# Hybrid attention layer, second query group: normalisation three slots behind its projection, copy, low part and transposition five slots behind it

## Chip, cores and metric

The kernel runs on one core of a Trainium2 chip. The metric is the device time of one launch in microseconds (us), as a median over runs; lower is better. Engines are named as the profile names them: PE (matrix multiply) and PEld (its weight load), DVE (vector), ACT (activation), POOL (general purpose) and SP, whose queue issues most of the transfers.

## The reference

One layer over 1024 tokens of width 1024. After an RMS normalisation, one projection gives the columns of two head groups and their gates. Group A is attention with 8 query heads on 2 key/value heads; its queries and keys are normalised per head and turned by rotary tables. Group B is attention in a neighbourhood window with a learned bias. What matters here is how the queries of group A come about:

```python
h = _rmsnorm(x, norm_gain[l])
proj = h @ w_in[l]
q_a, k_a, v_a, g_a, q_b, k_b, v_b, g_b = jnp.split(proj, split_at, axis=-1)
q_a = _rmsnorm(q_a.reshape(b, s, A_HEADS, HEAD_DIM), q_norm_a[l])
...
q_a = q_a * cos + _rotate_half_axial(q_a) * sin
...
o_a = _gqa_blocked(q_a, k_a, v_a) * jax.nn.silu(g_a)
```

The gated outputs of both groups go through an output projection, are added to x and normalised.

## The kernel before

**Tiling.** All columns are cut into 17 weight groups of 256 columns (13 of the input projection, 4 of the output projection). Float32 operands are split into a high and a low float16 part, and each product is three matmuls. A projection tile is two blocks of 128 tokens by 256 columns in one PSUM bank: 48 matmuls of 128x256, given out in eight chunks of six (`proj_pair`, `chunks`, L494). The four tiles of a group are called tile 0 to tile 3 here. The projection tiles use two PSUM buffers in turn, so a tile's first chunk waits until the tile two before it has been read out.

**The order of the work.** `Flow.step` makes one *slot*. In a slot it runs what was booked for "pre", then the slot's attention work, then "mid", the vector jobs, "post", and a number of projection chunks (`fill`). `at(delay, pos, fn)` books work for a later slot. Nine slots of eight chunks come first. Then come 64 slots, numbered 0 to 63 here, each with one *unit* of group A: one head and 128 queries. Slot i makes the scores of unit i in PSUM (L725, L727; two buffers in turn), the row minimum on DVE (L732), the exponential on ACT (L734), the float16 copy on ACT (L735), the low part on DVE (L740, in the slot after) and a transposition by SP (L745); five slots later PE multiplies with the values (L757 to L759). Slots 0 to 3 carry five chunks each, later ones about 4.2. In what prints of the program `s_1_2` and `nm_1_2` belong to unit 6 (block 1, head 2), `s_2_0` to unit 8, and the digits at the end of a name are serial numbers.

Each engine works through its own instructions in order. Until slot 5 the order on ACT, DVE, POOL and SP is chosen by a scheduler; from slot 6 on (`HAND`) instructions stand as they are written. PE's order is written out throughout.

**The second query group** (weight group 2, `QA + 1`; heads 4 to 7, first used in slot 32). Its tile 0 ends in the slot before slot 0, tile 1 in slot 1, tile 2 in slot 3 and tile 3 in slot 4. Per tile, `norm_rope` books:

- `a`, one slot later: two reads out of PSUM on ACT (L541, L542)
- `b`, one slot later: sums and scale on DVE (L545, L546) and a power on POOL (L547)
- `c`, two slots later: the product with that power on DVE (L551), two half products with the sine table on POOL (L555), the product with the cosine table on DVE (L558), the sum on POOL (L559)

and `qa_gen` books, four slots later, the float16 copy on ACT (L574), the low part on DVE (L575) and the transposition on SP (L578).

**Work that shares the queues.** Weight groups 3 and 4 make the queries of group B; their tiles are read out by L628 (ACT) and L633 (DVE). Group 3's tile 0 ends in slot 6, and its tile 2, which takes the same PSUM buffer, begins with the last chunk of slot 8. A weight group is scaled before it is split: squares on ACT (L362), a sum over partitions on PE (L378), a factor from that sum on DVE (L380), a power on POOL (L381), then the high part on ACT (L404) and the low part on DVE (L409). For weight group 4 this falls into slots 7 to 9. PE's wait for the scores of unit i is on the exponential of unit i-2 (same buffer).

## Time and profile before

| what | value |
|---|---|
| median of 3 runs | 566.72 us (564.27 to 571.57) |
| profiled execution | 566.36 us |
| its span, first to last instruction | 564.5 us |
| PE busy | 515.5 us, 91% of the span |
| DVE busy | 446.0 us, 79% |
| ACT busy | 367.8 us, 65% |
| POOL busy | 157.2 us, 28% |

The span is what the engines' rows cover; the profiled execution took 1.86 us more than that. A row of the timeline gives the start, the busy time, engine, line, operation, output and inputs with shapes, how many instructions were merged, and in brackets the idle time before it with the engine that ended it. A row of the windows view gives, for a stretch of the span, the busy time of each engine with its count of instructions, the clock granted to PE (1.00 is full), and the use of the DMA engines.

### The profile page before, as it was taken

What the parts mean: (1) busy time and instruction counts of PE and PEld (TensorE: products, weight loads), DVE (VectorE), ACT (ScalarE), POOL (GpSimd) and SP (SyncE); (2) the same over time, 40 slices, a digit from 0 to 9 for tenths busy, and PEclk for the clock granted to TensorE, in tenths of its full rate; (3) what the DMA queues carried; (4) which work ended last, traced back from release to release, by engine and by line L of the source; (5) the groups of instructions that cost most, each with busy time, mean ns of one, the idle gap of its engine ahead of it and who ended that gap; (6) DMA issues with size and microseconds to landing.
All of it is one profiled execution on the core that took longest, in us unless ns stands there. A gap on an engine that the chain in (4) does not pass through costs nothing.

```text
span 564.5 us, 13778 instructions
## 1 busy us (share of the span) xinstructions
PE 515.5 (91%) x5583; PEld 402.4 (71%) x5583; DVE 446.0 (79%) x911; ACT 367.8 (65%) x583; POOL 157.2 (28%) x181
## 2 busy tenths in 40 slices
PE   2577989989999999999999999999998889998994
PEld 0456877767887555568888888887776667788883
DVE  4588788989887988778789887588987798988532
ACT  5546456958787759587696886367777568663211
POOL 2395887670000000000000022433821231224000
PEclk9979999999999999999999999999999998999998
DMA  8999549789999999998999899436586599996612
GB/s 242 220 181 234 122 71 210 125 143 191 203 228 174 175 216 193 193 187 173 211 197 180 189 165 214 129 68 132 105 188 105 117 255 230 181 154 139 215 38 75
DMA packets 244513, 95.47 MB, mean 169 GB/s; under 512 B 235489, under 2 KB 236001, under 8 KB 242530
## 3 DMA queue, kind: packets, MB, share of 16 engines
q1 hardware_dynamic: 240850, 73.89, 71.8%
q0 software_dynamic: 3312, 19.92, 12.2%
q8 instruction: 43, 0.70, 0.5%
q10 hardware_dynamic: 288, 0.79, 0.5%
q14 instruction: 20, 0.16, 0.1%
HBM read 29.56 MB, written 4.19 MB: 60 GB/s over the span
## 4 chain that ended last, share of the span: by engine, by line
PE 51%; DVE 9%; ACT 8%; issue 5%; DMA 4%; SPq 0%; POOL 0%; DVEq 0%; POOLq 0%; ACTq 0%
PE pj L494 19%; PE kb L494 7%; PE pjb L494 5%; PE s L725 4%; PE s L727 4%; ACT rq L838 3%; PE sb L494 3%; PE pv L758 3%; DMA ar<-ar 3%; PE pv L759 3%; PE pv L757 3%; ACT ar L840 3%; DVE ar L836 2%; DVE ar L845 2%; DMA x2b<-in_x_dram 1%
## 5 line engine op out<-in xcount | busy, mean ns | idle before, releaser
L494 PEld LDWEIGHTS <-hT 128*128 128x128 f16 x2112 | 204.9, 100 | 58.8 <-issue 16.2
L494 PE MATMUL pj<-whl,hT 128*128 128x256 f16 x1680 | 201.6, 278 | 20.9 <-DMA hT<-ar 7.8
L734 ACT ACTIVATE ar<-s,nm,sm 128x1024 f32<-128x1024 f32 x64 | 76.9, 1202 | 56.6 <-DVE nm L732 56.3
L732 DVE CUSTOM_DVE_ANT_0 ar<-s,sm 128x1024 bf16<-128x1024 f32 x64 | 82.0, 1281 | 33.9 <-PE s L727 33.6
L494 PEld LDWEIGHTS <-ar 128*128 128x128 f16 x768 | 74.6, 99 | 11.7 <-issue 2.6
L740 DVE TENSOR_TENSOR ar<-ar 128x1024 f16<-128x1024 f32 x64 | 79.5, 1242 | 1.4 <-ACT ar L735 1.4
L735 ACT ACTIVATE ar<-ar 128x1024 f16<-128x1024 f32 x64 | 67.6, 1057 | 2.1 <-DVE sum L764 0.3
L838 ACT ACTIVATE rq<-ar,nm 128x384 f32<-128x384 f32 (+1 forms) x64 | 34.1, 580 | 38.4 <-DVE nm L836 37.7
L494 PE MATMUL pjb<-whl,ar 128*128 128x256 f16 x408 | 47.4, 273 | 0.0
L494 PE MATMUL kb<-hT,whl 128*128 128x512 f16 x192 | 44.5, 379 | 0.0
L409 DVE SCALAR_TENSOR_TENSOR whl<-raw,sm,whl 128x512 f16<-128x512 f32 x52 | 38.7, 770 | 2.8 <-ACT whl L404 2.8
L758 PE MATMUL pv<-va,ar 128*128 128x64 f16 x384 | 40.1, 194 | 0.0
L757 PE MATMUL pv<-va,ar 128*128 128x65 f16 x384 | 40.1, 193 | 0.0
L759 PE MATMUL pv<-va,ar 128*128 128x65 f16 x384 | 39.9, 192 | 0.0
L757 PEld LDWEIGHTS <-ar 128*128 128x128 f16 x384 | 35.7, 97 | 5.5 <-issue 0.3
L758 PEld LDWEIGHTS <-ar 128*128 128x128 f16 x384 | 35.5, 97 | 5.5 <-issue 0.3
L725 PE MATMUL s<-kTa,rq 128*128 128x512 f16 x128 | 38.5, 383 | 0.4 <-ACT ar L734 0.4
L212 POOL DMA_DIRECT2D raw<-in_w_dram x11 | 6.7, 607 | 113.0 <-ACT ar L735 89.0
L845 DVE SCALAR_TENSOR_TENSOR ar<-rq,ar 128x768 f16<-128x768 f32 (+1 forms) x32 | 30.7, 959 | 7.9 <-ACT ar L840 7.5
L879 POOL TENSOR_TENSOR ar<-ar,qkg 128x256 f32<-128x256 f32 x16 | 18.5, 1157 | 65.0 <-DVE qkg L877 63.7
L759 PEld LDWEIGHTS <-ar 128*128 128x128 f16 x384 | 35.5, 99 | 0.0
L404 ACT ACTIVATE whl<-raw,sm 128x512 f16<-128x512 f32 x52 | 34.0, 709 | 1.4 <-POOL sm L381 1.4
(174 smaller groups left out, 978.4 us busy)
## 6 DMA issues: line engine op xcount, KB each, us to landing
raw<-in_w_dram POOLq DMA_DIRECT2D x11, 1024.0 KB, 7.7
raw<-in_wo_dram POOLq DMA_DIRECT2D x4, 1024.0 KB, 6.3
ar<-in_x_dram SPq DMA_DIRECT2D x7, 512.0 KB, 6.3
khh<-ar SPq DMA_DIRECT2D x16, 128.0 KB, 3.4
x2b<-in_x_dram POOLq DMA_DIRECT2D x4, 512.0 KB, 6.9
x<-in_x_dram POOLq DMA_DIRECT2D x4, 512.0 KB, 6.2
out_dram<-x2b SPq DMA_DIRECT2D x8, 256.0 KB, 4.2
out_dram<-x SPq DMA_DIRECT2D x7, 256.0 KB, 2.9
```

The source lines that it names most:

```text
L409: dve.scalar_tensor_tensor(wp[g][1][:, q], raw[g][:, q], col(S_ + g), wp[g][0][:, q], op0=OP.mult, op1=OP.subtract)
L494: pe.matmul(*o[0], **o[1])
L725: pe.matmul(s[:, c * 512:(c + 1) * 512], q, kTa[:, 4 * c:4 * c + 4, hh], start=True, stop=False)
L732: dve.tensor_tensor_reduce(out=hl[:, 1].bitcast(BF16), in0=s, in1=col(SHA).to_broadcast([P, 1024]), scale=col(NSA), scalar=3e38, op0=OP.ad ...
L734: act.activation(p32, s, AF.Exp, bias=nm, scale=col(SCA))
L735: at(0, "mid", lambda: act.activation(hl[:, 0], p32, AF.Copy))
L740: dve.tensor_tensor(hl[:, 1], p32, hl[:, 0], op=OP.subtract)
L757: pe.matmul(o, pt[:, kt], va[:, kt, hh, v_hi], start=kt == 0, stop=False)
L758: pe.matmul(o[:, :D], pt[:, kt], va[:, kt, hh, v_lo], start=False, stop=False)
L759: pe.matmul(o, pt[:, 8 + kt], va[:, kt, hh, v_hi], start=False, stop=kt == 7)
L838: act.activation(p32[:, e], t[:, e], AF.Exp, bias=nm, scale=-1.0)
L845: dve.scalar_tensor_tensor(hl[:, 1], p32, 2.0 ** 14, hl[:, 0], op0=OP.mult, op1=OP.subtract)
```

## The change

Two delays grow by one slot for the second query group alone: `c` is booked three slots behind the projection instead of two, and copy, low part and transposition five instead of four. No instruction is added, removed or altered.

```diff
         at(1, "pre", a)
         at(1, "post" if g == QA + 1 else "mid", b)
-        at(2 if g == QA + 1 else 1, "post", c)
+        at(3 if g == QA + 1 else 1, "post", c)
         done(qn)
...
             def fin(q):
-                d = 4 if hh else 2
+                d = 5 if hh else 2
                 at(d, "pre", lambda: act.activation(stg[:, :, :, a:a + D], q, AF.Copy))
```

PE's instructions stand in the same order as before. On the other engines rows move between slots 2 and 10.

The first place is ACT from the exponential of unit 4 to that of unit 6 (slots 4 to 6). Before:

```order
L734 ACTIVATE ar<-s_1_0_1090,nm_1_0_1095,sm 128x1024
L574 ACTIVATE ar<-ar 128x8x64
L541 ACTIVATE ar<-pj_3_1059 128x512
L542 ACTIVATE ar<-pj_3_1059 128x512
L735 ACTIVATE ar<-ar 128x1024
L734 ACTIVATE ar<-s_1_1_1135,nm_1_1_1140,sm 128x1024
L735 ACTIVATE ar<-ar 128x1024
L734 ACTIVATE ar<-s_1_2_1209,nm_1_2_1214,sm 128x1024
```

Now:

```order
L734 ACTIVATE ar<-s_1_0_1083,nm_1_0_1088,sm 128x1024
L542 ACTIVATE ar<-pj_3_1051 128x512
L574 ACTIVATE ar<-ar 128x8x64
L362 ACTIVATE va,wss_2_937<-raw_933 128x512
L735 ACTIVATE ar<-ar 128x1024
L734 ACTIVATE ar<-s_1_1_1134,nm_1_1_1139,sm 128x1024
L362 ACTIVATE va,wss_3_938<-raw_933 128x512
L735 ACTIVATE ar<-ar 128x1024
L734 ACTIVATE ar<-s_1_2_1202,nm_1_2_1207,sm 128x1024
```

Two squares of weight group 5 (L362) have moved in, from a place some three slots earlier; L541 of tile 3 has moved ahead of unit 4's exponential.

The second place is DVE from the low part of unit 5 (the first L740) to the row minimum of unit 8. Before:

```order
L740 TENSOR_TENSOR ar<-ar 128x1024
L551 TENSOR_TENSOR ar<-ar,nt_3_1129 128x512
L558 TENSOR_TENSOR ar<-ar,tabs 128x512
L732 ISA ar,nm_1_3_1281<-s_1_3_1276,sm 128x1024
L732 ISA nm_1_3_1281 128x1
L740 TENSOR_TENSOR ar<-ar 128x1024
L575 TENSOR_TENSOR ar<-ar 128x8x64
L633 SCALAR_TENSOR_TENSOR ar<-pj_0_1180,ar 128x2x64 x4
L380 TENSOR_SCALAR wss_0_871<-pv_101 128x1
L732 ISA ar,nm_2_0_1360<-s_2_0_1355,sm 128x1024
```

Now:

```order
L740 TENSOR_TENSOR ar<-ar 128x1024
L575 TENSOR_TENSOR ar<-ar 128x8x64
L551 TENSOR_TENSOR ar<-ar,nt_2_1050 128x512
L558 TENSOR_TENSOR ar<-ar,tabs 128x512
L732 ISA ar,nm_1_3_1275<-s_1_3_1270,sm 128x1024
L732 ISA nm_1_3_1275 128x1
L740 TENSOR_TENSOR ar<-ar 128x1024
L633 SCALAR_TENSOR_TENSOR ar<-pj_0_1172,ar 128x2x64 x4
L551 TENSOR_TENSOR ar<-ar,nt_3_1129 128x512
L558 TENSOR_TENSOR ar<-ar,tabs 128x512
L380 TENSOR_SCALAR wss_0_871<-pv_101 128x1
L732 ISA ar,nm_2_0_1357<-s_2_0_1352,sm 128x1024
```

Ahead of L633 the same kinds of rows stand as before, but L551 and L558 are now tile 2's; tile 3's pair has moved behind L633 and stands ahead of L380, the factor of weight group 4.

The third place is POOL from the power of tile 1 to the power of weight group 4 (L381). Before:

```order
L547 TENSOR_TENSOR nt_1_973<-nt_1_973,mh 128x8
L555 TENSOR_TENSOR ar<-ar,tabs 128x8x32 x2
L559 TENSOR_TENSOR ar<-ar 128x512
L547 TENSOR_TENSOR nt_2_1058<-nt_2_1058,mh 128x8
L555 TENSOR_TENSOR ar<-ar,tabs 128x8x32 x2
L559 TENSOR_TENSOR ar<-ar 128x512
L547 TENSOR_TENSOR nt_3_1129<-nt_3_1129,mh 128x8
L555 TENSOR_TENSOR ar<-ar,tabs 128x8x32 x2
L559 TENSOR_TENSOR ar<-ar 128x512
L381 TENSOR_TENSOR sm<-wss_0_871,mh 128x1
```

Now:

```order
L547 TENSOR_TENSOR nt_1_968<-nt_1_968,mh 128x8
L555 TENSOR_TENSOR ar<-ar,tabs 128x8x32 x2
L547 TENSOR_TENSOR nt_2_1050<-nt_2_1050,mh 128x8
L559 TENSOR_TENSOR ar<-ar 128x512
L547 TENSOR_TENSOR nt_3_1129<-nt_3_1129,mh 128x8
L555 TENSOR_TENSOR ar<-ar,tabs 128x8x32 x2
L559 TENSOR_TENSOR ar<-ar 128x512
L555 TENSOR_TENSOR ar<-ar,tabs 128x8x32 x2
L559 TENSOR_TENSOR ar<-ar 128x512
L381 TENSOR_TENSOR sm<-wss_0_871,mh 128x1
```

The powers of tiles 2 and 3 have moved ahead of their neighbours' products, and L381 still follows tile 3's L555 and L559, which on DVE now start behind L633. On ACT, L404 of weight group 4 still stands ahead of the exponential of unit 8, with a copy of tile 2 (L574, tile 3's before) ahead of both. On SP each L578 has moved behind one or two later transpositions of units.

## The prediction

> **What bounds the kernel now.** I read the windows of the trace first, to see where PE does not work, then PE's timeline there, and then the timelines of the engines it waits for. A window's columns are its length and the busy time of PE, PEld, DVE, ACT and POOL, then PE's granted clock.

> ```profile
> 120.00:130.00 10.00, 7.28 (x73) 5.26 (x70) 9.93 (x19) 6.65 (x9) 4.54 (x4) 0.83 0.77 146
> 130.00:140.00 10.00, 10.00 (x124) 8.36 (x122) 9.96 (x19) 7.60 (x10) 0.64 (x1) 1.00 1.13 188
> ...
> 300.00:350.00 50.00, 50.00 (x628) 41.15 (x626) 43.21 (x73) 36.34 (x44) 6.87 (x10) 1.00 0.97 191
> ```

> From 130 to 350 us, first and last window shown, PE is never idle, so whatever PE loses or gains before 130 arrives whole at 350, and I let it run through to the end. In 120 to 130 PE is busy for 7.28 of 10 us while DVE is busy for 9.93. This hole lies in the slots that the change rearranges.

> ```profile
> 102.20 0.59 PE L725 MATMUL s<-kTa,rq 128*128 128x512 f16 x2 [0.44 <-ACT ar L734]
> ...
> 114.17 0.59 PE L725 MATMUL s<-kTa,rq 128*128 128x512 f16 x2
> ...
> 118.49 0.59 PE L725 MATMUL s<-kTa,rq 128*128 128x512 f16 x2
> ...
> 120.09 2.78 PE L494 MATMUL pj<-whl,hT 128*128 128x256 f16 x24
> 125.59 1.44 PE L494 MATMUL pj<-whl,hT 128*128 128x256 f16 x6 [2.72 <-DVE wss L380]
> 126.82 1.06 PE L725 MATMUL s<-kTa,rq 128*128 128x512 f16 x2
> ...
> 132.07 0.59 PE L725 MATMUL s<-kTa,rq 128*128 128x512 f16 x2
> ...
> 136.29 0.59 PE L725 MATMUL s<-kTa,rq 128*128 128x512 f16 x2
> ```

> An L725 opens each PE slot; 118.49 is unit 8's, 132.07 unit 10's. A slot with four chunks takes 136.29 - 132.07 = 4.22 us; one with the sum over weight group 4 (L378) 118.49 - 114.17 = 4.32; a fifth chunk adds a quarter of the 2.62 between a group of 24 and the next row, 0.66. Slot 8 has five chunks and should take 4.88; it takes 8.33. Slot 9 takes 5.25 instead of 4.22. Together 3.45 + 1.03 = 4.48 us are lost: 2.72 of waiting, and about 1.76 because PE restarts slowly:

> ```profile
> 126.00:128.00 2.00, 2.00 (x8) 1.03 (x7) 2.00 (x4) 1.82 (x3) 0.15 (x1) 0.50 1.08 202
> ```

> The granted clock is 0.50 there. The chunk that waited is the first of group 3's tile 2. The row names L380, but the buffer is freed by the four L633 just ahead of it:

> ```profile
> 101.76 1.28 DVE L732 CUSTOM_DVE_ANT_0 ar<-s,sm 128x1024 bf16<-128x1024 f32 x1
> ...
> 106.55 1.28 DVE L732 CUSTOM_DVE_ANT_0 ar<-s,sm 128x1024 bf16<-128x1024 f32 x1
> ...
> 115.25 1.27 DVE L732 CUSTOM_DVE_ANT_0 ar<-s,sm 128x1024 bf16<-128x1024 f32 x1
> ...
> 119.22 0.69 DVE L551 TENSOR_TENSOR ar<-ar,nt 128x512 f32<-128x512 f32 x1 [1.54 <-POOL nt L547]
> 119.94 0.69 DVE L558 TENSOR_TENSOR ar<-ar,tabs 128x512 f32<-128x512 f32 x1
> 120.55 1.28 DVE L732 CUSTOM_DVE_ANT_0 ar<-s,sm 128x1024 bf16<-128x1024 f32 x1
> ...
> 121.75 1.22 DVE L740 TENSOR_TENSOR ar<-ar 128x1024 f16<-128x1024 f32 x1
> 122.90 1.75 DVE L575 TENSOR_TENSOR ar<-ar 128x512 f16<-128x512 f32 x1
> 124.58 0.87 DVE L633 SCALAR_TENSOR_TENSOR ar<-pj,ar 128x128 f16<-128x128 f32 x4
> 125.37 0.14 DVE L380 TENSOR_SCALAR wss<-pv 128x1 f32<-128x1 f32 x1
> ```

> The L732 shown are those of units 3, 4, 6 and 7. DVE stands still for 1.54 us at tile 3's L551, which waits for POOL's power, and spends 1.75 on an L575 that takes 0.69 elsewhere. So L633 comes too late.

> **The change part by part.** It adds no instruction; everything follows from the order.

> *What goes.* Ahead of L633 stands tile 2's L551 instead of tile 3's. Tile 2's power was ready long before, so the 1.54 goes; and ahead of unit 6's L732 stand an L575, an L551 and an L558 less. If that were all, L633 would be in time and PE would get back 4.48 us.

> *What comes first: unit 4's exponential is later.* ACT's rows:

> ```profile
> 98.78 0.63 ACT L362 ACTIVATE va<-raw 128x512 bf16<-128x512 f32 x1
> ...
> 99.39 1.05 ACT L735 ACTIVATE ar<-ar 128x1024 f16<-128x1024 f32 x1
> ...
> 107.87 1.21 ACT L734 ACTIVATE ar<-s,nm,sm 128x1024 f32<-128x1024 f32 x1 [1.09 <-DVE nm L732]
> 108.97 0.62 ACT L574 ACTIVATE ar<-ar 128x512 f16<-128x512 f32 x1
> 109.49 0.59 ACT L541 ACTIVATE ar<-pj 128x512 f32<-128x512 f32 x1
> 109.97 0.60 ACT L542 ACTIVATE ar<-pj 128x512 f32<-128x512 f32 x1
> 110.45 1.06 ACT L735 ACTIVATE ar<-ar 128x1024 f16<-128x1024 f32 x1
> 111.39 1.22 ACT L734 ACTIVATE ar<-s,nm,sm 128x1024 f32<-128x1024 f32 x1
> ...
> 126.18 2.56 ACT L404 ACTIVATE whl<-raw,sm 128x512 f16<-128x512 f32 x4 [1.42 <-POOL sm L381]
> 128.65 1.19 ACT L734 ACTIVATE ar<-s,nm,sm 128x1024 f32<-128x1024 f32 x1
> ```

> From start to start an L734 takes 1.10, L574 0.52, L542 0.48, L735 0.94, L362 0.61 and four L404 2.47; on DVE an L740 takes 1.15, L551 0.72, L558 0.61, L732 1.20, four L633 0.79. Unit 3's and unit 4's L732 start 4.79 apart; between them there is now one L740 and one small L546 (0.2) more and an L575 (0.69) less: 5.45. Unit 3's own L732 has an L575 newly ahead of it, with two L362 taken off ACT in that place: I put it at 102.2 to 102.5. Unit 4's L732 then starts at 107.7 to 108.0 (was 106.55), its exponential 1.32 later as now, ending at 110.2 to 110.5. PE, which no longer waits the 0.44 at 102.20, wants that buffer at 109.5: a wait of 0.7 to 1.0 that is not there today.

> *Unit 6.* ACT runs L734, L542, L574, L362 and L735 from 109.0 to 109.3 on: 1.10 + 0.48 + 0.52 + 0.61 + 0.94 = 3.65, so 112.7 to 113.0, up to 0.5 more where L574 waits for tile 1's sum, which on POOL now stands behind tile 2's power. An L740 later, at 113.9 to 114.7, unit 6's L732 starts (was 115.25). ACT ends L734, L362 and L735 of unit 5 at 115.4 to 116.1.

> *L633.* From there DVE does L740, L575, L551, L558, L732, L740: 1.15 + 0.69 + 0.72 + 0.61 + 1.20 + 1.15 = 5.52. L633 starts at 120.9 to 121.6 and ends by 122.4, where PE reaches the waiting chunk at about 123.2 (L725 at 110.3 to 110.6, then 4.22 and 4.32 to 119.0, and 4.2 into slot 8). The old wait goes.

> *What is late next.* Tile 3's L551 and L558, which stood ahead, now stand behind L633, and POOL can start tile 3's L555 and L559 only then. Behind these on POOL stands L381, behind it on ACT the four L404, behind them unit 8's exponential, and behind that the scores of unit 10 on PE. POOL's rows:

> ```profile
> 120.04 1.86 POOL L555 TENSOR_TENSOR ar<-ar,tabs 128x256 f32<-128x256 f32 x2 [0.86 <-ACT ar L628]
> 121.97 2.13 POOL L559 TENSOR_TENSOR ar<-ar 128x512 f32<-128x512 f32 x1
> 125.59 0.56 POOL L381 TENSOR_TENSOR sm<-wss,mh 128x1 f32<-128x1 f32 x1 [1.49 <-DVE wss L380]
> ```
> ```profile
> 104.44 2.77 POOL L555 TENSOR_TENSOR ar<-ar,tabs 128x256 f32<-128x256 f32 x2 [0.87 <-DVE ar L551]
> 107.29 1.27 POOL L559 TENSOR_TENSOR ar<-ar 128x512 f32<-128x512 f32 x1
> ```

> Today L559 is over at 124.1, 1.49 us before L381 can start, so L381 waits only for L380. Now: L551 starts at 121.7 to 122.4 and takes 0.72; L555 takes 1.86 to 2.77, L559 1.27 to 2.13, L381 0.56: 126.1 to 128.6. With L404 (2.47) and the exponential (1.19) unit 8's buffer is free at 129.8 to 132.3, and up to 1.06 later if an L575 is again held up as at 122.90 (1.75 instead of 0.69). PE wants it at 119.0 + 4.88 + 4.22 = 128.1. So there is a new wait of 1.7 to 5.2 us, about as long as the one that goes. L380 itself moves to 123.0 to 123.8 and ends by 124, and PE's first product of the second block with the values waits for it at 124.7: no cost, with 0.7 us to spare.

> *The sum*, by the start of unit 10's scores, today 132.07: 129.8 to 133.4. L575 and L558 on DVE and tile 2's and 3's L555 and L559 on POOL now run against each other just there, so I take the upper part, 132.0. Then PE restarts slowly, as at 126 today, which I price with the same 1.76, less about 0.2 because slot 10 has no fifth chunk. That is 132.0 - 132.07 + 1.6 = +1.5 us; from -0.7 (129.8, slow restart) or -2.3 (129.8, no slow restart) to +2.9. The first, short wait (0.7 to 1.0) is inside, since PE waits for unit 8 in any case. Span 564.5 + 1.5 = 566.0; the profiled execution takes 1.86 us more than its span and lies 0.36 under the median shown, so I predict **567.9 us**, with 564.1 to 569.3 as this case's own range. That is within 2% (11.3 us) of 566.72, about what a measurement of this kernel can tell from no change.

> What speaks on the slow restart: PE's idle of 2.72 us was followed by a clock of 0.50. [...]

> **The rivals.**

> *The stall goes and no other comes*: -4.48, that is 561.9 us. It needs unit 8's exponential over by 128.1, so L381 at 123.8 and tile 3's L551 by 119.9 at the latest, about as early as today, though it now stands behind L633. It could be had if POOL's rows were shorter than any shown. Halfway lies a wait too short to lower the clock: -2.3, 564.1.

> *POOL and DVE hold each other up* (slower). L575's 1.75 starts at 122.90 inside L559's 2.13, and both are long against 0.69 and 1.27. If each of the pairs that now meet does this, L575 and L558 ahead of L633 give 1.06 + 0.5, and tile 3's rows take their longest:

> ```profile
> L555 POOL TENSOR_TENSOR ar<-ar,tabs x24: 449/730/1710, 39.8 to 121.2; 128x256 f32<-128x256 f32 x16, 128x128 f32<-128x128 f32 x8
> L559 POOL TENSOR_TENSOR ar<-ar x12: 723/1266/2266, 41.4 to 122.0; 128x512 f32<-128x512 f32 x8, 128x256 f32<-128x256 f32 x4
> ```

> Two of 1.71 and one of 2.27 are 0.8 more than I counted: 132.3 + 1.6 + 0.8 = 134.7, so +2.6 + 1.6 = +4.2, 570.6 us. It decides as soon as L381 starts after 127.8 (then unit 10 starts after 132.07). [...]

> *The change does nothing that can be seen*: the wait moves from slot 8 to slot 10 at the same length. Tile 0's L551 does not even move in the order. Then 4.48 goes and 4.48 comes: 566.4 us.

> **How the numbers follow.** New wait a little longer than the old: 0.42, 567.9. No new stall: 0.17, 561.9 to 564.1. POOL and DVE in each other's way: 0.21, 570.6. Nothing: 0.20, 566.4. All four lie within 2%; beyond it only something I don't see. The runs shown spread over 7.3 us, so I add some 2 us on either side of 564.1 and 570.6: 562.0 to 573.0. Faster by over 2% (under 555.4) 0.02, slower by over 2% (over 578.1) 0.03, within 0.95.

> **What would show it.** In the changed profile the first chunk of group 3's tile 2 has no wait on DVE, and tile 3's L551 no wait on POOL; PE's wait named L734 lies before unit 10's scores and is 2 to 5 us long, with a granted clock near 0.5 right behind it, and a short one before unit 6's. L404 waits 2 to 4 us for POOL's L381, and POOL works without a gap from tile 3's L555 to L381. I am wrong if L381 still starts right behind L380 with POOL idle before it; if PE shows no wait over 1.5 us between 105 and 140; or if the total differs while these waits are as said, in which case the difference comes from behind 350 us.

## The result and the profile after

| | before | changed |
|---|---|---|
| median of 13 runs each | 566.68 us (564.27 to 571.57) | 572.71 us (571.26 to 588.16) |
| profiled execution | 566.36 us | 572.71 us |
| its span | 564.5 us | 570.9 us |

The ratio of the changed kernel to the one before is 1.0085, 95% interval 1.0056 to 1.0114: slower by less than 2%. The median is 4.8 us over the 567.9 forecast and just inside its upper bound of 573.0. Two later comparisons of the same two programs gave 1.0043 (1.0009 to 1.0078) and 1.0063 (1.0023 to 1.0103). Medians here and below are of all runs; the ratios leave out runs over 1.5% above the fastest of their program, and the profiled execution of n_after3 below (579.21 us) is one of those, so that it enters no mean.

First the windows of the changed kernel's trace, with the columns as in the prediction:

```profile
120.00:130.00 10.00, 10.00 (x124) 8.37 (x122) 9.93 (x18) 4.48 (x6) 7.81 (x6) 1.00 1.01 198
130.00:140.00 10.00, 6.44 (x58) 4.84 (x57) 8.14 (x16) 7.92 (x11) 1.20 (x2) 0.83 0.64 111
...
300.00:350.00 50.00, 50.00 (x625) 41.14 (x623) 44.68 (x75) 35.53 (x42) 6.17 (x9) 1.00 0.95 188
```

The hole has moved. 120 to 130 us, where PE lost 2.72 us, is full; 130 to 140 has PE busy for 6.44 of 10 us. PE's timeline of the changed kernel, the first scores of units 6, 10, 11 and 12:

```profile
113.60 0.59 PE L725 MATMUL s<-kTa,rq 128*128 128x512 f16 x2 [1.36 <-ACT ar L734]
...
134.94 0.59 PE L725 MATMUL s<-kTa,rq 128*128 128x512 f16 x2 [3.56 <-ACT ar L734]
...
140.76 0.59 PE L725 MATMUL s<-kTa,rq 128*128 128x512 f16 x2
...
145.08 0.59 PE L725 MATMUL s<-kTa,rq 128*128 128x512 f16 x2
```

Both waits are on an exponential (L734) of the unit two before. Slot 10 takes 140.76 - 134.94 = 5.82 us, 1.6 more than a slot with four chunks, and behind the wait the clock is low for one stretch:

```profile
134.94:135.40 0.46, 0.46 (x3) 0.22 (x3) 0.00 (x0) 0.46 (x1) 0.00 (x0) 1.00 0.01 2
135.40:138.80 3.40, 3.40 (x34) 2.46 (x33) 2.79 (x7) 3.37 (x6) 0.00 (x0) 0.50 0.09 19
138.80:142.00 3.20, 3.20 (x36) 2.52 (x35) 3.20 (x5) 1.86 (x3) 0.00 (x0) 0.99 1.13 210
```

What unit 8's exponential waits for, on DVE, POOL and ACT:

```profile
124.22 0.87 DVE L633 SCALAR_TENSOR_TENSOR ar<-pj,ar 128x128 f16<-128x128 f32 x4
125.01 0.97 DVE L551 TENSOR_TENSOR ar<-ar,nt 128x512 f32<-128x512 f32 x1
126.01 0.69 DVE L558 TENSOR_TENSOR ar<-ar,tabs 128x512 f32<-128x512 f32 x1
...
127.89 1.22 DVE L740 TENSOR_TENSOR ar<-ar 128x1024 f16<-128x1024 f32 x1
129.03 1.76 DVE L575 TENSOR_TENSOR ar<-ar 128x512 f16<-128x512 f32 x1
```
```profile
126.11 1.86 POOL L555 TENSOR_TENSOR ar<-ar,tabs 128x256 f32<-128x256 f32 x2 [0.68 <-ACT ar L574]
128.05 2.19 POOL L559 TENSOR_TENSOR ar<-ar 128x512 f32<-128x512 f32 x1
130.20 1.01 POOL L381 TENSOR_TENSOR sm<-wss,mh 128x1 f32<-128x1 f32 x1
```
```profile
131.24 2.56 ACT L404 ACTIVATE whl<-raw,sm 128x512 f16<-128x512 f32 x4 [5.14 <-POOL sm L381]
133.70 1.18 ACT L734 ACTIVATE ar<-s,nm,sm 128x1024 f32<-128x1024 f32 x1
```

L633 comes in time and tile 3's L551 behind it waits for nothing. POOL then works through tile 3's L555, L559 and weight group 4's L381 without a gap, ACT stands for 5.14 us before L404, and unit 8's exponential ends as PE's wait ends.

**Where the 6.4 us of span are.** Compared from PE's weight loads, which stand in the same order in both programs, unit 3's scores start 2.72 us later (100.18 against 97.46), before any row that the change moved has been waited for. From there to unit 12's scores, the stretch that the change rearranges, it takes 145.08 - 100.18 = 44.90 us against 43.15: +1.75. From unit 12's scores to 300 us of the trace before nothing differs (0.01), and another 1.95 arise in group B, between 430 and 500 us of the trace before. Two of PE's waits there in the changed kernel, and one each of two later profiles of the program before (n_before, then n_before2):

```profile
452.20 0.32 PE L815 MATMUL sb<-khh,qTb 128*128 128x384 f16 x1 [4.13 <-DVE nm L836]
...
472.48 0.20 PE L865 MATMUL pvb<-ar 128*128 128x65 f16 x1 [3.03 <-DMA ar<-ar]
```
```profile
448.15 0.48 PE L815 MATMUL sb<-khh,qTb 128*128 128x384 f16 x1 [4.13 <-DVE nm L836]
```
```profile
465.37 0.24 PE L865 MATMUL pvb<-ar 128*128 128x65 f16 x1 [5.45 <-DMA ar<-ar]
```

In the first profile of the program before, the wait on L836 was 2.74 us and none was on L865. So neither the longer wait on L836 nor a transfer that is late at L865 is anything that the change made; the unchanged program has both, in some executions.

### The profile page after: what moved, and what is told of

It is laid out like the page before. It is cut to its first block, busy times and chain, and to the rows that moved or that the text cites. A ratio compares the mean times of both kernels' runs of the same rounds, so it can differ in the third digit from the quotient of the medians.

```text
span 570.9 us, 13780 instructions
## 1 busy us (share of the span) xinstructions
PE 515.9 (90%) x5583; PEld 402.8 (71%) x5583; DVE 445.7 (78%) x911; ACT 367.4 (64%) x583; POOL 155.4 (27%) x181
## 4 chain that ended last, share of the span: by engine, by line
PE 51%; ACT 10%; DVE 7%; issue 5%; DMA 4%; POOL 0%; DVEq 0%; POOLq 0%; ACTq 0%
PE pj L494 18%; PE kb L494 7%; PE pjb L494 6%; PE s L727 4%; PE s L725 4%; ACT rq L838 4%; DMA ar<-ar 4%; PE sb L494 3%; ACT ar L840 3%; PE pv L758 3%; PE pv L759 3%; PE pv L757 3%; DVE ar L836 2%; DVE ar L845 2%; ACT rest L362 1%
## 5 line engine op out<-in xcount | busy, mean ns | idle before, releaser
L494 PEld LDWEIGHTS <-hT 128*128 128x128 f16 x2112 | 204.6, 99 | 57.7 <-DMA hT<-ar 17.6
L494 PE MATMUL pj<-whl,hT 128*128 128x256 f16 x1680 | 202.0, 279 | 19.9 <-DMA hT<-ar 9.9
L734 ACT ACTIVATE ar<-s,nm,sm 128x1024 f32<-128x1024 f32 x64 | 76.9, 1201 | 55.0 <-DVE nm L732 52.9
L732 DVE CUSTOM_DVE_ANT_0 ar<-s,sm 128x1024 bf16<-128x1024 f32 x64 | 81.9, 1281 | 33.4 <-PE s L727 33.1
L494 PEld LDWEIGHTS <-ar 128*128 128x128 f16 x768 | 75.2, 100 | 12.6 <-issue 2.8
L740 DVE TENSOR_TENSOR ar<-ar 128x1024 f16<-128x1024 f32 x64 | 79.3, 1240 | 3.6 <-ACT ar L735 3.6
L735 ACT ACTIVATE ar<-ar 128x1024 f16<-128x1024 f32 x64 | 67.6, 1057 | 2.1 <-DVE ar L740 0.3
L494 PE MATMUL pjb<-whl,ar 128*128 128x256 f16 x408 | 47.4, 273 | 0.0
L494 PE MATMUL kb<-hT,whl 128*128 128x512 f16 x192 | 44.5, 379 | 0.0
L725 PE MATMUL s<-kTa,rq 128*128 128x512 f16 x128 | 38.0, 379 | 4.9 <-ACT ar L734 4.9
L404 ACT ACTIVATE whl<-raw,sm 128x512 f16<-128x512 f32 x52 | 34.0, 709 | 5.1 <-POOL sm L381 5.1
```

What stands on the lines that cost most here:

```text
L494: pe.matmul(*o[0], **o[1])
L725: pe.matmul(s[:, c * 512:(c + 1) * 512], q, kTa[:, 4 * c:4 * c + 4, hh], start=True, stop=False)
L732: dve.tensor_tensor_reduce(out=hl[:, 1].bitcast(BF16), in0=s, in1=col(SHA).to_broadcast([P, 1024]), scale=col(NSA), scalar=3e38, op0=OP.ad ...
L734: act.activation(p32, s, AF.Exp, bias=nm, scale=col(SCA))
L735: at(0, "mid", lambda: act.activation(hl[:, 0], p32, AF.Copy))
L740: dve.tensor_tensor(hl[:, 1], p32, hl[:, 0], op=OP.subtract)
```

## The experiments

Each ratio is from runs on the same chip as those of the program before. "Stretch" is the time from the start of unit 3's scores to the start of unit 12's in the profiled execution, "waits" are PE's in it.

| run | ratio to before (95%) | median | stretch | waits in it |
|---|---|---|---|---|
| the two programs first compared: before | 1 | 566.68 | 43.15 | 0.44 and 2.72 |
| changed | 1.0085 (1.0056 to 1.0114) | 572.71 | 44.90 | 1.36 and 3.56 |
| n_before | 0.9994 (0.9955 to 1.0034) | 567.41 | 42.72 | 2.74 |
| n_before2 | 1.0014 (0.9981 to 1.0047) | 569.24 | 43.00 | 0.48 and 2.73 |
| n_after | 1.0043 (1.0009 to 1.0078) | 571.31 | 42.08 | 2.31 |
| n_after2 (one run) | - | 571.81 | 44.58 | 1.36 and 3.55 |
| n_after3 | 1.0063 (1.0023 to 1.0103) | 572.34 | 43.30 | 1.17 and 3.54 |
| c3_f4 | 1.0023 (0.9986 to 1.0060) | 571.26 | 44.50 | 0.48 and 3.94 |
| c2_f5 | 0.9974 (0.9931 to 1.0017) | 568.31 | 38.00 | none |
| t3_6 | 0.9966 (0.9931 to 1.0001) | 565.17 | 38.00 | none |
| t3_6b | 0.9966 (0.9937 to 0.9995) | 566.69 | 38.00 | none |
| sq5 | 1.0029 (0.9993 to 1.0066) | 569.35 | 41.85 | 2.08 |
| c2_f5_sq5 | 0.9980 (0.9944 to 1.0015) | 567.18 | 38.00 | none |
| t3_6_sq5 | 0.9962 (0.9928 to 0.9996) | 566.04 | 38.00 | none |

The median of before was 568.64 us beside n_before, n_after, c3_f4 and c2_f5 (35 runs), 567.96 beside t3_6, sq5, c2_f5_sq5 and n_after2 (29), and 568.42 beside the other four (35).

The stretch without any wait is 38.00 us, five times out of five. Every other entry is 38.00 plus the waits plus 0.6 to 2.1 us, which I put down to the low clock behind the waits for the most part: 38.00 + 0.44 + 2.72 leaves 1.99 for before, 38.00 + 1.36 + 3.56 leaves 1.98 for the changed kernel.

### The parts of the change alone

The products one slot later, the copies in their old place:

```diff
-        at(2 if g == QA + 1 else 1, "post", c)
+        at(3 if g == QA + 1 else 1, "post", c)
```

> Only the normalisation (c) is moved, to three slots; copy, low part and transposition stay at four. ACT's order is then that of the kernel before, and tile 3's products stand behind L633 and ahead of L381 as in the change. Theory of the prediction (L381 behind tile 3's products costs): the wait before unit 10's scores is there with 3 to 5 us, the one before unit 6's is gone, and the middle stage takes 44.0 to 45.5 us; ratio 1.002 to 1.008. Rival (the later copies on ACT cost, with the wait before unit 6's scores as their mark): the middle stage takes 42.5 or less, ratio 0.998 or less.

Measured: the long wait before unit 10 is there, as long as with the whole change, and none before unit 6. The two rows of tile 2's and tile 3's copy on ACT, and PE's wait:

```profile
122.37 0.63 ACT L574 ACTIVATE ar<-ar 128x512 f16<-128x512 f32 x1 [3.65 <-POOL ar L559]
...
129.41 0.63 ACT L574 ACTIVATE ar<-ar 128x512 f16<-128x512 f32 x1 [3.68 <-POOL ar L559]
```
```profile
133.63 1.01 PE L725 MATMUL s<-kTa,rq 128*128 128x512 f16 x2 [3.94 <-ACT ar L734]
```

So the later products suffice to make the new wait. That it is L381 which passes it on, this run doesn't show: tile 3's copy on ACT (the second L574) waits for the same L559 itself and stands ahead of L404. PE also waits 1.28 us before unit 3 here, ahead of the stretch; there ACT waited 4.07 us for weight group 5's load, of which more below.

The copies one slot later, the products in their old place:

```diff
-                d = 4 if hh else 2
+                d = 5 if hh else 2
```

> Only copy, low part and transposition are moved, to five slots; the normalisation stays at two. Tile 3's products stay ahead of L633, so L381 waits only for L380, and tile 2's L575 goes behind L633. Theory of the prediction: the wait before unit 6's scores (1.4 us) is there, none before unit 10's, at most 1 us in slot 8, and the middle stage takes 40.0 to 41.5 us; ratio 0.994 to 0.997. Rival (the later copies cost): 44 to 45 us as in the change, ratio 1.003 or more. Theory B above (any such change makes the rest slower by 4 us): ratio 1.002 or more with a middle stage of 41.

Measured: the old wait goes and no other comes, not even the expected one before unit 6. L381 starts early, and PE is never idle:

```profile
121.44 2.14 POOL L559 TENSOR_TENSOR ar<-ar 128x512 f32<-128x512 f32 x1
123.54 0.56 POOL L381 TENSOR_TENSOR sm<-wss,mh 128x1 f32<-128x1 f32 x1
```
```profile
120.00:130.00 10.00, 10.00 (x122) 8.15 (x121) 9.93 (x21) 8.60 (x13) 4.02 (x4) 1.00 1.11 177
130.00:140.00 10.00, 10.00 (x138) 8.25 (x137) 9.96 (x22) 7.17 (x8) 1.21 (x2) 1.00 1.03 196
```

Of the two lines of the change, the second by itself takes the stall away, and the first makes the new one. The stretch is 5.15 us shorter than in the program before, better than expected; the time is not. That no wait stands before unit 6 belongs to this execution: ACT waited only 0.90 us for a load that had made it wait 2.62 us in the trace before (more on it below). ACT's order is that of the changed program, which has that wait in its three executions with a late load, so I would expect it here too with a late load; no profile shows it.

### L381 ahead of tile 3's products

The change as it is, with tile 3 alone another slot later:

```diff
-        at(3 if g == QA + 1 else 1, "post", c)
+        at((4 if up == 3 else 3) if g == QA + 1 else 1, "post", c)
...
-                d = 5 if hh else 2
+                d = (6 if up == 3 else 5) if hh else 2
```

> The changed program with tile 3's last step and its copy, low part and transposition one slot later still (normalisation four slots behind its projection, copy six behind), the other three tiles as in the change. That puts the power L381 on POOL ahead of tile 3's products L555 and L559 and behind those of tile 2. Theory (the long wait before unit 10 comes from L381 standing behind two tiles' products): L381 starts some 4 us earlier against unit 8's scores, the high parts L404 follow it, and the wait before unit 10 falls from 2.3 to 3.6 us to under 0.5 us; in its place up to 1.5 us of waiting in slot 10's last chunk, which needs tile 3's transposition. From unit 3's scores to unit 12's: 38 to 41 us instead of 42.1 and 44.9 in the two executions of the changed program. Rival (the wait comes from the exponentials being late on ACT and DVE as a whole, and the power's place decides little): the wait before unit 10 stays at 2 us or more and the stretch at 42 to 45 us.

POOL's rows, and ACT's high parts behind them:

```profile
119.62 2.13 POOL L559 TENSOR_TENSOR ar<-ar 128x512 f32<-128x512 f32 x1
121.72 0.56 POOL L381 TENSOR_TENSOR sm<-wss,mh 128x1 f32<-128x1 f32 x1
127.30 1.86 POOL L555 TENSOR_TENSOR ar<-ar,tabs 128x256 f32<-128x256 f32 x2 [5.02 <-ACT ar L735]
```
```profile
121.79 0.63 ACT L574 ACTIVATE ar<-ar 128x512 f16<-128x512 f32 x1
122.33 2.54 ACT L404 ACTIVATE whl<-raw,sm 128x512 f16<-128x512 f32 x4
```

L381 stands between tile 2's L559 and tile 3's L555, L404 no longer waits for it, and the wait is gone, with nothing in its place (I had allowed 1.5 us in slot 10's last chunk). This settles that L381's place behind tile 3's products makes the wait before unit 10: the changed program has 2.31 us of it even in the execution with the least waiting for the load, 1.05 us (n_after, below), and here ACT waited 1.68.

### What sets the size of the wait

The changed program unchanged, three times more:

> The changed kernel, unchanged, for a second profile. Both theories: the middle stage 44.9 within 0.5, with the wait of 3 to 4 us before the scores of unit 10 and one of 1.4 before unit 6's. Theory A: the first and last stage lie elsewhere than 100.2 and 425.8, by a us or two, on either side. Theory B: again 100.2 and 425.8 within 0.5. Median 572 to 573 under both, ratio 1.008 to 1.011.

> The changed program itself, once more, for a third profile. Theory of the load: the sum of the waits before unit 6 and before unit 10 goes with ACT's wait for weight group 5's load ahead of unit 1's exponential, as 4.9 us with 2.71 and 2.3 us with 1.05 did: about the wait for the load plus 1.2 to 2.2 us. Rival: no such relation.

> The changed program itself, for a fourth profile and a second ratio on the chip of the other kernels. Theory of the load: if ACT waits over 2 us for weight group 5's load ahead of unit 1's exponential, two or three waits of 4.9 us or more in all and 44 to 45 us from unit 3's scores to unit 12's; if under 1.5 us, one wait of about 2.3 us and 42 us. The ratio to the program before between 1.003 and 1.009.

The second profile had one wait and not two, 42.08 us instead of the 44.9 that both theories gave. n_after2 came out as expected (4.91 us for the two waits, against 4.7 to 5.7), n_after3 a little below (4.71 us, and 43.30 in the stretch). The difference begins at ACT's squares of weight group 5 (L362), which stand ahead of unit 1's exponential and wait for that group's load. ACT and PE of n_after, then of n_after2, then of n_after3:

```profile
94.27 0.63 ACT L362 ACTIVATE va<-raw 128x512 bf16<-128x512 f32 x1 [1.05 <-DMA raw<-in_w_dram]
```
```profile
130.89 0.68 PE L725 MATMUL s<-kTa,rq 128*128 128x512 f16 x2 [2.31 <-ACT ar L734]
```
```profile
96.21 0.63 ACT L362 ACTIVATE va<-raw 128x512 bf16<-128x512 f32 x1 [3.53 <-DMA raw<-in_w_dram]
```
```profile
98.08 0.59 PE L725 MATMUL s<-kTa,rq 128*128 128x512 f16 x2 [0.65 <-ACT ar L734]
111.50 0.59 PE L725 MATMUL s<-kTa,rq 128*128 128x512 f16 x2 [1.36 <-ACT ar L734]
132.83 1.01 PE L725 MATMUL s<-kTa,rq 128*128 128x512 f16 x2 [3.55 <-ACT ar L734]
```
```profile
95.84 0.63 ACT L362 ACTIVATE va<-raw 128x512 bf16<-128x512 f32 x1 [2.49 <-DMA raw<-in_w_dram]
```
```profile
111.12 0.59 PE L725 MATMUL s<-kTa,rq 128*128 128x512 f16 x2 [1.17 <-ACT ar L734]
132.45 0.59 PE L725 MATMUL s<-kTa,rq 128*128 128x512 f16 x2 [3.54 <-ACT ar L734]
```

In the first profile of the changed kernel that row of L362 waited 2.71 us. Its rows show how the lateness reaches PE at unit 6:

```profile
101.74 0.69 DVE L545 TENSOR_REDUCE nt<-ar 128x8 f32<-128x512 f32 x1 [2.04 <-ACT ar L542]
...
111.03 1.27 DVE L732 CUSTOM_DVE_ANT_0 ar<-s,sm 128x1024 bf16<-128x1024 f32 x1
```
```profile
98.31 0.63 ACT L362 ACTIVATE va<-raw 128x512 bf16<-128x512 f32 x1 [2.71 <-DMA raw<-in_w_dram]
...
112.34 1.20 ACT L734 ACTIVATE ar<-s,nm,sm 128x1024 f32<-128x1024 f32 x1 [3.33 <-DVE nm L732]
```

L362 late, L542 behind it late, DVE's L545 waits for it for 2.04 us, unit 4's row minimum behind L545 (L732 at 111.03) is late, and so is its exponential, for which PE waits before unit 6. With 1.05 us for the load there is no wait before unit 6, and 2.31 before unit 10; with 2.49, 2.71 and 3.53 there are 1.17, 1.36 and 1.36 before unit 6, and then always 3.54 to 3.56 before unit 10, since PE has by then been held back to the pace of ACT and DVE. As a sum: 2.3 us for 1.05, and 4.7, 4.9 and 5.6 (with the 0.65 ahead of the stretch) for 2.49, 2.71 and 3.53.

To test it, the squares one slot later, behind the exponentials of units 1 and 2:

```diff
-            squares(g, 4)
+            squares(g, 5 if g == 5 else 4)
```

> The changed program with the squares of weight group 5 (L362 on ACT) one slot later, so that their wait for the load stands behind the exponentials of units 1 and 2 and not ahead of them. Theory (the size of the new waits is set by how long ACT waits for that load: 2.71 us where there were two waits of 1.36 and 3.56 us, 1.05 us where there was one of 2.31 us): ACT doesn't wait for the load, no wait before unit 6's scores, the one before unit 10's at 2.5 us or less, and 40 to 42.5 us from unit 3's scores to unit 12's in whatever execution; the median 1 to 3 us below that of the changed program (about 568 to 570). Rival (the row maxima on DVE are late by DVE's own queue, and the load has no part in it): a wait of over 1 us before unit 6 or one of over 3 us before unit 10, as in the first profile, and the median of the changed program within 1 us.

PE's only wait in the stretch, and the clock behind it:

```profile
131.36 0.87 PE L725 MATMUL s<-kTa,rq 128*128 128x512 f16 x2 [2.08 <-ACT ar L734]
```
```profile
132.40:134.80 2.40, 2.40 (x29) 1.91 (x28) 2.37 (x6) 2.37 (x5) 0.00 (x0) 0.50 0.00 0
```

The wait before unit 6 is gone, and the one before unit 10 is the short one, as the theory has it. But this execution can't decide between the two. From issue to landing the load of weight group 5 took 8.0 us in it, as in n_after (8.1), which has no wait before unit 6 either; in the three executions of the changed program with that wait it took 9.5 to 10.5. And the median, 569.35, lies under those of the changed program (571.31 to 572.71), but the intervals of the ratios overlap. A later run is the better test: t3_6_sq5, whose rows up to unit 6 stand in the order of sq5's. Its load took 10.8 us, PE doesn't wait before unit 6, and unit 4's exponential waits 0.94 us for its row minimum instead of 3.33:

```profile
106.72 1.21 ACT L734 ACTIVATE ar<-s,nm,sm 128x1024 f32<-128x1024 f32 x1 [0.94 <-DVE nm L732]
```

So the load, through the place of the squares, makes the wait before unit 6. One reservation stays: with the squares later, the scheduler also put one L545 on DVE ahead of a row minimum. That the wait before unit 10 stays short with a late load, no profile of sq5 shows.

The program before, for the same question:

> The kernel before, unchanged, as a control and for a second profile. Three stages are compared in every profile: up to the scores of unit 3 (97.46 us before, 100.18 changed), from there to the scores of unit 12 (43.15 and 44.90), and from there to the end (423.9 and 425.8). Theory A (only the slots 2 to 10 differ, the rest is spread between executions): the first and the last stage move here by a us or two although nothing is changed, the middle one by under 0.5. Theory B (the changed program is slower outside these slots too): the first stage stays within 0.5 us of 97.5 and the last within 0.5 of 423.9. Ratio 1.00 under both.

> The program before, unchanged, for a third profile: whether its stretch from unit 3's scores to unit 12's is as constant as the two profiles say (43.1 and 42.7 us). Theory (its one wait, in slot 8, hangs on POOL's products and not on the load): 42 to 43.5 us whatever ACT's wait for weight group 5's load. Rival (the load sets it as well): under 41 us in an execution with a short wait for the load, which would explain why the programs with 38.0 us there don't come out five microseconds ahead. Ratio 0.996 to 1.004.

```profile
96.24 0.63 ACT L362 ACTIVATE va<-raw 128x512 bf16<-128x512 f32 x1 [3.06 <-DMA raw<-in_w_dram]
```
```profile
126.34 1.44 PE L494 MATMUL pj<-whl,hT 128*128 128x256 f16 x6 [2.73 <-DVE wss L380]
```

With 2.0, 2.62 and 3.06 us of waiting for the load the old wait is 2.74, 2.72 and 2.73: in this range it does not hang on the load, and the program before has 42.7 to 43.2 us in the stretch each time. The changed order has taken a wait that did not move with the load and put one in its place that does. The rival isn't out, though: none of the three executions of the program before had a short wait for the load, as those of c2_f5 (0.90 us), t3_6 (1.68) and t3_6b (1.12) had. As to the stages, n_before moved by 0.9, -0.4 and 0.7 us with nothing changed, and n_after's first and last stage (98.95 and 424.2) lie over 1 us from the first profile's; theory B, by which they stay within 0.5, is out.

### Versions without a wait, and what they bring

c2_f5_sq5 is c2_f5 with the later squares, t3_6b is t3_6 once more, t3_6_sq5 is t3_6 with the later squares; the edits are those shown above.

> Normalisation left two slots behind the projection, copy, low part and transposition five behind, and the squares of weight group 5 one slot later. Theory (all that the two programs lose lies in the waits of slots 6 to 10, the rest of their difference is spread): no wait over 0.5 us from unit 3's scores to unit 12's, 37.5 to 39 us for that stretch against 42.7 and 43.2 us in the program before, and a time of 562 to 566 us, 0.990 to 0.998 of it. Rival (what is won in the middle stage is given back behind it, as the later stages are set by transfers): the stretch as short, and the stretch from unit 12's scores to the end longer by as much, with the ratio between 0.998 and 1.004.

> The program with tile 3 one slot later still, once more unchanged. Its stretch from unit 3's scores to unit 12's was 38.0 us against 43.1 and 42.7 in the program before, but its median only 2.8 us under that program's (ratio 0.9966). Theory (the five microseconds of the middle stage come through in full, and the rest was spread between executions): ratio near 0.991 this time. Rival (part of what the middle stage wins is not won at the end, as waits in front of it and in group B differ between the programs): the ratio again at 0.995 to 0.998, with 38.0 us in the middle.

> Tile 3 one slot later still, and weight group 5's squares one slot later too. Theory (the load's landing lengthens the middle stage only through ACT; with tile 3's products behind the power there is room for it): no wait over 0.5 us and 38.0 us in the middle whatever the load does; the time is that of the same program with the squares in their old place, within 1.5 us, or up to 1.5 us less if in some executions the late load made a wait there. Rival (the squares in their later place hold the exponentials of units 5 and 6): a wait of 0.5 us or more before unit 6 or 7 and a time 1 us or more longer.

All three have 38.00 us in the stretch. Against t3_6b the later squares of t3_6_sq5 change nothing that can be measured (566.69 and 566.04). Both are faster than the program before, by 0.34% and 0.38%, with intervals below 1, and their intervals lie wholly below those of the changed program. But 0.34 to 0.38% is about 2 us, and the stretch is 5 us shorter. t3_6b's ratio lies where its rival had it, and 0.991 outside its interval: part of the gain does not arrive. c2_f5_sq5's 0.9980 stands on the border of theory and rival, and its interval holds most of both.

Where the other 3 us are isn't settled. The medians of the programs with the copies five slots behind are all higher than their stretch makes them, against three stretches of 42.7 to 43.2 for the program before:

| program | stretch against before | median against before, by its ratio |
|---|---|---|
| changed (means of three profiles and three ratios) | +0.9 | +3.6 |
| sq5 | -1.1 | +1.6 |
| c2_f5 | -5.0 | -1.5 |
| c2_f5_sq5 | -5.0 | -1.1 |
| t3_6, t3_6b, t3_6_sq5 | -5.0 | -1.9 to -2.2 |

c3_f4, with the copies in their old place, doesn't show this (+1.5 in the stretch and 1.28 ahead of it, +1.3 by its ratio). Between unit 12's scores and 300 us of the trace before, all profiles but n_after3's agree, except for one transfer wait of about 1 us behind the stretch in c2_f5 and half of that in c2_f5_sq5, so it isn't there. Unit 3's scores start at 97.46 to 98.31 in three profiles of before and at 97.36 to 100.18 in nine of the programs with the copies five behind (n_after3 left out), and from 300 us of the trace before to the last of PE's weight loads it is 256.6 to 261.8 and 256.6 to 262.3 us: a spread of several us in both, in PE's waits for transfers (3.03 and 5.45 us at L865 above) and in the clock (0.94 to 0.97 from 440 to 500 us), and too few profiles to say whether the means differ. By these profiles the nine lose 1.0 us on average ahead of the stretch and nothing behind 300. The stretches compared above are not alike either: three of the five of 38.00 us come from programs with the squares in their old place and executions with an early load, all three of the program before from executions with a late one. Some of the 5 us may be that. Whether chance makes the rest, or something that the order does, no run tells; it stays open.

## Why the prediction was right in its mechanism and short in its size

- **The old wait goes.** Right. Taking off the 2.72 us that the profile of the changed kernel is late ahead of the stretch, L633 starts at 124.22 - 2.72 = 121.50 (forecast 120.9 to 121.6) and tile 3's L551 at 122.29 (121.7 to 122.4).
- **L381 comes late behind tile 3's products.** Right, at the late end: it is over at 130.20 + 1.01 - 2.72 = 128.49 (126.1 to 128.6). POOL has no gap from L555 to L381. ACT's wait for it was 5.14 us, more than the 2 to 4 I gave.
- **Unit 10's scores.** 134.94 - 2.72 = 132.22, forecast 132.0. t3_6, where L381 stands ahead of tile 3's products and the wait is gone, shows the cause.
- **POOL and DVE hold each other up.** In part, as the choice of the upper end assumed. L575 took 1.76 beside L559's 2.19, and L381, which I priced at 0.56, took 1.01: it started at 130.20, while L575 ran until 130.79, and in c2_f5 and t3_6, with no such neighbour, it takes 0.56. L555's first product took 1.18 us at 126.11, beside an L558 of the usual 0.69, and its second 0.71, beside L732. No run changes such a neighbour alone, so that the neighbour makes these times is my reading of the rows.
- **The slow restart, +1.6.** Right for slot 10, which takes 5.82 - 4.22 = 1.60 more; over the whole stretch 1.98 are left beside the waits. The clock was 0.50 for one stretch of 3.40 us.
- **The clock behind a short wait.** The prediction had one row for it, 2.72 us followed by 0.50. Waits of 2.31 us (n_after) and 2.08 us (sq5) were followed by 0.50 too, one of 3.54 us in n_after3 by 1.00: the length of the wait alone does not say it, and that is what I left out. No run shows a new wait of about 1.7 us with the clock left full, on which -2.3 and 564.1 rest; what the runs showed is a wait of 1.36 us in the changed kernel with a clock of 1.00 from 111.2 to 120 us.
- **The sum for the stretch, +1.5.** Right for the first profile (+1.75), and an accident of it: other executions gave -1.07 and +1.43 against 43.15, because the wait's size goes with a load. I took ACT's lateness from the one profile of before, where the load was 2.62 us late, as if it were fixed. That term was mis-sized by up to 2.6 us. The same lateness made the wait before unit 6 1.36 us instead of 0.7 to 1.0, and 0 in n_after.
- **"Whatever PE loses or gains before 130 arrives whole at 350, and I let it run through to the end."** The first half holds (159.34 us from unit 12's scores to 300 in before and changed kernel). The second half is the step that failed. It set everything ahead of the stretch and behind 350 us to zero, and that is where the first profile has 2.72 + 1.95 of its 6.4 us, none of it made by the change as far as the rows show. About 3 us of the medians' difference aren't in the profiled stretches either; where they are stays open. The same step would have promised 5 us for t3_6, which brings 2. That the measured time lies inside the range 562.0 to 573.0 owes something to the 2 us added on either side for the spread of runs: the sum's own range ended at 569.3.
- **The rivals.** "The stall goes and no other comes" did not happen, though half of the change does it (c2_f5). The slower rival, 570.6, came nearest to the medians, but not for its reason: L575 (1.76 instead of 0.69) and L381 (1.01 instead of 0.56) add 1.5 us, and L381 starts at 130.20 - 2.72 = 127.48, ahead of the 127.8 that was to decide for it.

## What to carry to other kernels

When a step is moved a slot later, ask for every engine's queue what now stands ahead of the next thing that PE waits for: here a power of 0.56 us went behind 4 us of products that nobody was waiting for, and moving that one pair of products further back took the whole wait away. Moving two coupled steps together can hide that one of them does the good and the other the harm; run each alone. A wait read from one profile has a fixed size only if the chain behind it has no transfer in it, two versions are best compared in executions where that transfer was equally late, and a stretch that gets shorter by 5 us has not made the kernel faster by 5 us until the medians say so.

## What the runs showed of the hardware

**Behind these waits the clock was low for about 3.4 us, and not just from the wait's end.** Behind waits of 2.08, 2.31, 2.72 and 3.56 us (sq5, n_after, before and the changed kernel) PE had a clock of 0.50 for about 3.4 us: in the changed kernel from 0.49 us after the wait's end, in before from 0.06 us ahead of it, in n_after, where the wait ended at 130.89, from 131.3 to 134.7:

```profile
131.30:134.70 3.40, 3.40 (x33) 2.48 (x32) 2.75 (x7) 3.37 (x6) 0.00 (x0) 0.50 0.07 15
```

In n_after2 the low clock began while PE still waited (the row before the end of its wait at 132.83), and 1.67 us are left beside its waits, against 1.98 in the first profile of the changed kernel. In n_after3 the clock stayed at 1.00 behind a wait of 3.54 us; in the first two of three windows of 3.41 us PE was idle for 46 and 58%. First n_after2's row, then the three windows of n_after3:

```profile
132.00:132.50 0.50, 0.00 (x0) 0.00 (x0) 0.50 (x2) 0.50 (x1) 0.00 (x0) 0.70 1.12 207
```
```profile
127.05:130.46 3.41, 1.85 (x17) 1.51 (x16) 2.95 (x6) 1.71 (x3) 1.67 (x2) 1.00 0.96 155
130.46:133.87 3.41, 1.42 (x23) 0.94 (x23) 2.01 (x4) 3.38 (x5) 0.00 (x0) 1.00 0.42 80
133.87:137.29 3.42, 3.31 (x38) 2.65 (x34) 3.42 (x8) 2.83 (x5) 0.00 (x0) 1.00 0.41 80
```

So the wait of 2.08 us in sq5 left 1.8 us more in the stretch, and those of 1.17 and 3.54 us in n_after3 only 0.6.

**The same load lands with a spread of 3 us.** From issue to landing weight group 5's load took 7.9 us (c2_f5) to 11.1 us (c3_f4), and ACT waited for it from 0.90 to 4.07 us at the same row. In six profiles (n_after, sq5, t3_6, t3_6b, c2_f5, c2_f5_sq5) it took under 9 us, in the other eight over 9, and the same six have a stretch of low clock from about 80 us that the others don't have (from 80 to 90 us 0.83 in n_after and c2_f5, 1.00 in before, the changed kernel, n_before and c3_f4). The waits behind which the clock drops there stand ahead of everything that the change moved. Whether the early load and the low clock hang together no run tells.
